# First-layer keys zero-padded to 128 rows, and conditioning products kept in one piece, in a two-layer transformer kernel

## The chip, the core and the metric

The kernel runs on one core of a Trainium2 chip. The metric is the device time of one execution in microseconds (us), from the kernel's start to its end; the time before is the median of three runs. The engines are named as in the profile: PE is TensorE with its matmuls, PEld is its weight load, DVE is VectorE, ACT is ScalarE, POOL is GpSimd, and SP issues the DMAs. PEclk is the clock that the throttle granted TensorE, as a share of full speed.

## What is computed

256 tokens of width 1024 pass two layers. Each layer has a mixer and an MLP, each with shift, scale and gate from a conditioning vector c. Cut to what the change touches:

```python
def ada_modulation(c, w, b):
    m = jax.nn.silu(c) @ w + b
    shift, scale, gate = jnp.split(m[:, None, :], 3, axis=-1)
    return shift, scale, 1.0 + gate

def mixer_ab(h, cos, sin, w_in, q_norm, w_uq, w_uiq, sinks, w_out):     # layer 0
    aq, ak, av, cq, bk, bv, bik, biw = _split_widths(h @ w_in, AB_WIDTHS)
    ...                                       # rotary embedding of queries and keys
    ya = swa_sink_attention(aq, ak, av, sinks)        # A: 8 heads, window 128, 2 key heads
    yb = dsa_attention(bq, bk, bv, biq, bik, iw)      # B: 8 heads, one key head, top 64 keys
    return jnp.concatenate([ya, yb], axis=-1) @ w_out
```

In dsa_attention an indexer first scores every key: `raw = einsum('bqhd,bsd->bhqs', iqb, ik)`, then relu, a weighted sum over 8 heads, and the 64 best keys for each query. A head has 64 numbers (HD = 64). Layer 1 has 16 ordinary heads (group C), which the change leaves as they are.

## The kernel before, in words

**Stages.** The projections of layer 0 (`group`, L615 and L635) accumulate over 8 tiles of 128 channels until about 48 us. Then the first mixer's attention runs, to about 150 us, beside the output projection `ps_out`; then the first MLP, layer 1's mixer, and the second MLP. Tokens are two blocks of 128, `b` = 0 and 1. Block 0 has 128 keys, block 1 has 256.

**Score products.** Queries and keys are transposed so that the 64 numbers of a head lie on partitions: even heads on rows 0 to 63 of a tile, odd heads on rows 64 to 127 (`half` = 0 or 1). The keys `akT`, `bkT` and `ikT` hold both halves in one tile. A product at L486 (`ps_s`, attention) or L759 (`ps_i`, indexer) takes the rows of one half of both operands, so it is a matmul of 64 rows. f32 matmuls are issued as two instructions each; the profile counts both.

**One step of attention** (`attend`) is a pair of heads: two products at L486, the mask and row minimum on DVE (L490, `negm`), Exp on ACT (L494), transposes on PE (L498), a copy on ACT (L500), and the products with the values (L505, `ps_pv`). The indexer's chain is L759 on PE, Relu on ACT (L761), and a sum on DVE (L764); `select` then runs 8 rounds of MAX and MATCH_REPLACE on DVE (L774, L775).

**Conditioning beside it.** Twelve pieces of the conditioning weights (`by_tensor`: the gate of the first half-layer, shift and scale of the second) are evaluated by PE (`ada_rows`). One piece is 8 matmuls at L334, 16 instructions, with 32 weight columns each: silu(c) in column 0 and zeros in 31, built once as `cT` of 128 x 8 x 32. The four column groups hold four partial sums; an ACT copy (L339) and two products with a column of ones (L350, `onec`) add them up. In PE's queue these products stand between the attention's own.

**What sets the order.** The tile framework's scheduler orders each engine's queue by priority, the program's order by default. `later(n)` raises the number of what is recorded inside it, so that it stands later; `ROWS_LATER` (30) is the number for `ada_rows`, L186. `st` interleaves the sides: A of block 0 beside the indexer, A of block 1 beside selection and B's queries, then B of both blocks beside `ps_out`. Weights come by DMA on SP in the order of `plan`, four buffers ahead of what has been taken.

**Buffers.** Rotary embedding writes the keys of B and the indexer into `kd`, one buffer of a tag of its own; most other work tiles of that size share the tag `r2` with 8 buffers. `ps_kd` is their transpose (L706), copied to `bkT` and `ikT` by L707 and L708.

## Time and profile before

| What | us |
|---|---|
| median of 3 runs (lowest, highest) | 728.42 (724.62, 729.69) |
| profiled execution, its own time | 719.67 |
| its span (first to last instruction) | 717.9 |
| PE busy | 674.9 (94%) |
| PEld busy | 543.8 (76%) |
| DVE busy | 473.1 (66%) |
| ACT busy | 336.2 (47%) |
| POOL busy | 67.7 (9%) |
| mean DMA rate | 211 GB/s |

The profile is of one execution. Its page gives busy time by engine, the span in 40 slices with PEclk, and groups of instructions by line. The stretch view gives, for each stretch of time, the busy time of every engine with its count of instructions in brackets, PEclk, the DMA engines' share and GB/s. The timeline gives start, length, engine, line, operation, tiles, rows x columns of the weights, shape of the streamed operand, count, and in square brackets the engine's idle time before it and what ended it. A length in the timeline runs to the modelled end of the last instruction, which overlaps the next; the distance from one start to the next start is the pace. The chain of waits shows the same work as non-overlapping pieces.

### The profile page before, as it was taken

The page shows a single profiled execution, that of the slowest core. Times are in us where ns is not written, and L with a number is a line of the kernel's source. Part 1 is how long each engine was busy: PE and PEld are TensorE (multiplying, and loading weights), DVE is VectorE, ACT ScalarE, POOL GpSimd, SP SyncE. Part 2 cuts the span into 40 slices and gives each one's busy share as a digit, 9 for nine tenths or more (in the row PEclk, how much of TensorE's full clock was granted, in tenths as well). Part 3 has the DMA queues.
Part 4 walks back from the last instruction along what each step waited for, and adds up shares of the span by engine and source line. Part 5 has one row for each costly group of instructions (what it writes and reads, how often), then busy time and mean ns, then how long its engine had stood idle before and what let it go on. Part 6 is the DMA issues. An engine that isn't in the chain of part 4 may idle for free.

```text
span 717.9 us, 9838 instructions
## 1 busy us (share of the span) xinstructions
PE 674.9 (94%) x3802; PEld 543.8 (76%) x3802; DVE 473.1 (66%) x858; ACT 336.2 (47%) x528; POOL 67.7 (9%) x85
## 2 busy tenths in 40 slices
PE   6998998999799999999978999999989999999994
PEld 3545555667689899898956877778779998989883
DVE  2855754626988877776497988854688754445537
ACT  3233333734465554545553444455546545555540
POOL 3010000003402000000043000000340010000004
PEclk9995857999999999999997999969999999999998
DMA  8991424760679898877444776731067765555301
GB/s 316 408 380 35 152 107 158 278 267 1 208 268 385 307 351 294 304 266 283 149 126 168 242 288 237 286 126 52 1 235 292 284 248 205 190 189 176 118 0 59
DMA packets 24385, 151.52 MB, mean 211 GB/s; under 512 B 2833, under 2 KB 3089, under 8 KB 8338
## 3 DMA queue, kind: packets, MB, share of 16 engines
q1 hardware_dynamic: 24194, 150.71, 57.3%
q8 instruction: 30, 0.49, 0.3%
q10 hardware_dynamic: 144, 0.18, 0.1%
q14 instruction: 17, 0.14, 0.1%
HBM read 149.83 MB, written 1.05 MB: 210 GB/s over the span
## 4 chain that ended last, share of the span: by engine, by line
PE 64%; issue 24%; DVE 7%; POOL 2%; DMA 1%; ACT 1%; SPq 0%; DVEq 0%; POOLq 0%; ACTq 0%
PE ps_m L236 16%; PE ps_m L234 16%; PE ps_m L235 16%; PE ps_g L615 3%; PE ps_s L486 2%; PE ps_ada L334 2%; PE ps_g L635 2%; PE ps_pv L505 2%; DVE wl L172 2%; PE ps_uq L727 1%; PE ps_i L759 1%; DMA early<-in_ada_dram 1%; DVE hTl L172 1%; PE ps_pt L498 1%; POOL x L588 1%
## 5 line engine op out<-in xcount | busy, mean ns | idle before, releaser
L172 DVE TENSOR_TENSOR wl<-w_w,wh 128x1024 fp32r<-128x1024 f32 x128 | 156.3, 1239 | 93.8 <-ACT wh L171 93.3
L171 ACT CAST wh<-w_w 128x1024 fp32r<-128x1024 f32 x128 | 131.1, 1052 | 154.8 <-PE ps_m L235 89.4
L234 PE MATMUL ps_m<-hTh,wh 128*128 128x256 f32 x448 | 126.7, 283 | 0.0
L236 PE MATMUL ps_m<-hTh,wl 128*128 128x256 f32 x448 | 126.6, 283 | 0.0
L235 PE MATMUL ps_m<-hTl,wh 128*128 128x256 f32 x448 | 126.6, 283 | 0.0
L234 PE MATMUL ps_m<-wh,uh 128*128 128x512 f32 x256 | 101.8, 398 | 0.0
L235 PE MATMUL ps_m<-wl,uh 128*128 128x512 f32 x256 | 101.3, 396 | 0.2 <-DVE wl L172 0.2
L236 PE MATMUL ps_m<-wh,ul 128*128 128x512 f32 x256 | 101.1, 396 | 0.0
L321 DVE CUSTOM_DVE_ANT_0 junk<-w_ada,cB,sm 128x1024 bf16<-128x1024 f32 x68 | 87.1, 1281 | 10.2 <-DMA w_ada<-in_ada_dram 9.4
L235 PEld LDWEIGHTS ps_m<-hTl,wh 128*128 128x128 f32 x448 | 85.7, 191 | 1.3
L234 PEld LDWEIGHTS ps_m<-hTh,wh 128*128 128x128 f32 x448 | 85.7, 191 | 1.2
L236 PEld LDWEIGHTS ps_m<-hTh,wl 128*128 128x128 f32 x448 | 85.7, 191 | 0.1
L236 PEld LDWEIGHTS ps_m<-wh,ul 128*128 128x128 f32 x256 | 48.2, 188 | 11.7 <-DVE ul L172 0.6
L234 PEld LDWEIGHTS ps_m<-wh,uh 128*128 128x128 f32 x256 | 48.3, 189 | 10.4 <-ACT uh L171 0.8
L235 PEld LDWEIGHTS ps_m<-wl,uh 128*128 128x128 f32 x256 | 48.2, 188 | 10.1 <-DVE wl L172 0.6
L236 PE MATMUL ps_c<-wh,hTl 128*128 128x512 f32 x96 | 39.8, 415 | 4.5 <-DVE hTl L172 4.5
L234 PE MATMUL ps_c<-wh,hTh 128*128 128x512 f32 x96 | 40.9, 426 | 3.2 <-ACT hTh L171 3.2
L235 PE MATMUL ps_c<-wl,hTh 128*128 128x512 f32 x96 | 39.5, 412 | 0.0
L171 ACT CAST wh<-w_ci 128x1024 fp32r<-128x1024 f32 x24 | 25.1, 1054 | 27.9 <-PE ps_c L236 20.1
L301 POOL TENSOR_TENSOR rs<-rs,mhalf 128x1 f32<-128x1 f32 x8 | 6.7, 832 | 333.1 <-DVE rs L573 333.1
L172 DVE TENSOR_TENSOR ul<-relu,uh 128x512 fp32r<-128x512 f32 (+1 forms) x36 | 24.8, 689 | 16.7 <-ACT uh L171 16.7
L494 ACT ACTIVATE prob<-prob,negm 128x128 f32<-128x128 f32 (+1 forms) x64 | 26.7, 453 | 18.5 <-DVE negm L490 18.5
(221 smaller groups left out, 1076.8 us busy)
## 6 DMA issues: line engine op xcount, KB each, us to landing
w_w<-in_w_dram SPq DMA_DIRECT2D x64, 1024.0 KB, 5.0
w_ada<-in_ada_dram SPq DMA_DIRECT2D x40, 1024.0 KB, 4.9
w_ci<-in_c_in_dram SPq DMA_DIRECT2D x12, 1024.0 KB, 5.0
w_ada<-in_ada_dram SPq DMA_DIRECT2D x12, 512.0 KB, 9.5
w_wo<-in_w_out_dram SPq DMA_DIRECT2D x4, 1024.0 KB, 5.6
w_co<-in_c_out_dram SPq DMA_DIRECT2D x4, 1024.0 KB, 4.9
w_g<-in_w_g_dram SPq DMA_DIRECT2D x8, 356.0 KB, 9.1
early<-in_ada_dram SPq DMA_DIRECT2D x4, 512.0 KB, 8.8
```

The source lines that it names most:

```text
L171: nc.scalar.copy(dh, src)
L172: nc.vector.tensor_sub(dl, src, dh.bitcast(F32))
L234: nc.tensor.matmul(ps, a[0], b[0], start=start, stop=False)
L235: nc.tensor.matmul(ps, a[0], b[1], start=False, stop=False)
L236: nc.tensor.matmul(ps, a[1], b[0], start=False, stop=stop)
L321: state[key, j] = nc.vector.tensor_tensor_reduce(out=junk, in0=w, in1=cB, scale=1.0, scalar=bias, op0=ALU.mult, op1=ALU.add, accum_out=m)
L334: m = nc.tensor.matmul(ps[g, :256], cT[:, k], w[:, 256 * k:256 * (k + 1)], start=k < 4, stop=k >= 4)
L486: nc.tensor.matmul(ps[:, j * 256:j * 256 + nk], qT[rows, p0 + j, b * P:(b + 1) * P], kT(p0 + j)[rows, :nk], start=True, stop=True)
L494: state["critical"] = nc.scalar.activation(pr[:, j, :nk], pr[:, j, :nk], AF.Exp, bias=negm[:, hd:hd + 1], scale=-1.0)
L505: state["pv"] = nc.tensor.matmul(pv[:, i * 65:(i + 1) * 65], flat[:, o:o + P], vv(kb, head(p0 + j, half)), start=(kb == 0), stop=(kb == b))
L615: nc.tensor.matmul(ps[b][:, :s.stop - s.start], hk[:, b * P:(b + 1) * P], w[:, s], start=k == 0, stop=k == KT - 1)
L635: nc.tensor.matmul(g1[b], hk[:, b * P:(b + 1) * P], parts["g1", k // 2][0][:, k % 2 * 512:k % 2 * 512 + 512], start=k == 0, stop=k == KT - 1)
```

## The change

Each key tile of layer 0 becomes two, one for each half, 128 rows high, with the other half's rows set to zero by POOL. Both operands of L486 (for A and B) and L759 then have 128 rows; the query rows of the wrong half meet zeros. Layer 1 keeps 64-row products. ACT fills the halves with copies of 64 partitions, two where there was one. `kd` moves to the tag `r2`. `cT` becomes 128 x 8, and a step of zero repeats each column 32 times in the weight load; all four column groups' 32 rows then hold the same partial sum, and a column `four`, which is one at rows 0, 32, 64 and 96, takes the place of `onec`. `ROWS_LATER` becomes 0.

```diff
-SPLITS_LATER, ADA_LATER, ROWS_LATER = 200, 300, 30
+SPLITS_LATER, ADA_LATER, ROWS_LATER = 200, 300, 0
...
-    cT = const.tile([P, KT, 32], F32, name="cT")
-    nc.gpsimd.memset(cT, 0.0)
-    nc.scalar.activation(cT[:, :, 0], sm[:, S_C:S_C + KT], AF.Silu)
-    onec = const.tile([P, 1], F32, name="onec")
-    nc.gpsimd.memset(onec, 1.0)
+    cT = const.tile([P, KT], F32, name="cT")
+    nc.scalar.activation(cT, sm[:, S_C:S_C + KT], AF.Silu)
...
+    four = const.tile([P, 1], F32, name="four")
+    nc.vector.tensor_reduce(out=four, in_=ident[:, ::32], op=ALU.add, axis=mybir.AxisListType.X)
...
-            m = nc.tensor.matmul(ps[g, :256], cT[:, k], w[:, 256 * k:256 * (k + 1)], start=k < 4, stop=k >= 4)
+            m = nc.tensor.matmul(ps[g, :256], cT[:, k:k + 1].to_broadcast([P, 32]), w[:, 256 * k:256 * (k + 1)], start=k < 4, stop=k >= 4)
...
-            nc.tensor.matmul(ps[:, 256 + j:257 + j], rows[:, j * P:(j + 1) * P], onec, start=True, stop=True)
+            nc.tensor.matmul(ps[:, 256 + j:257 + j], rows[:, j * P:(j + 1) * P], four, start=True, stop=True)
...
-                rows = slice(half * HD, (half + 1) * HD)
...
                 for j in range(2):
+                    rows, keys = kT(p0 + j, half)
                     nc.tensor.matmul(ps[:, j * 256:j * 256 + nk], qT[rows, p0 + j, b * P:(b + 1) * P],
-                                     kT(p0 + j)[rows, :nk], start=True, stop=True)
+                                     keys[rows, :nk], start=True, stop=True)
...
-    bkT = work.tile([P, 256], F32, name="bkT")
-    ikT = work.tile([P, 256], F32, name="ikT")
+    akT, bkT, ikT = ([work.tile([P, 256], F32, name=n + str(half)) for half in range(2)] for n in ("akT", "bkT", "ikT"))
+    for kT in (akT, bkT, ikT):
+        for half in range(2):
+            nc.gpsimd.memset(kT[half][(1 - half) * HD:(2 - half) * HD], 0.0)
...
-        kd = work.tile([P, 2, 2, HD], F32, name="kd", tag="kd", bufs=1)
+        kd = work.tile([P, 4, 2, HD], F32, name="kd", tag="r2", bufs=8)[:, :2]
...
-        nc.scalar.copy(bkT[:, q], ps[:, :P])
-        nc.scalar.copy(ikT[:, q], ps[:, P:2 * P])
+        for half in range(2):
+            rows = slice(half * HD, (half + 1) * HD)
+            nc.scalar.copy(ikT[half][rows, q], ps[rows, P:2 * P])
+        for half in range(2):
+            rows = slice(half * HD, (half + 1) * HD)
+            nc.scalar.copy(bkT[half][rows, q], ps[rows, :P])
...
-        to_T([kr[:, :2].rearrange("p h d -> p (h d)")], akT[:, b * P:(b + 1) * P].rearrange("p (n q) -> p n q", n=1))
+        ps = pc("ps_T")
+        nc.tensor.transpose(ps[:, :P], kr[:, :2].rearrange("p h d -> p (h d)"), ident)
+        for half in range(2):
+            rows = slice(half * HD, (half + 1) * HD)
+            nc.scalar.copy(akT[half][rows, b * P:(b + 1) * P], ps[rows, :P])
...
-                    nc.tensor.matmul(ps[:, j * 256:j * 256 + nk], iqT[rows, p0 + j, b * P:(b + 1) * P],
-                                     ikT[rows, :nk], start=True, stop=True)
+                    nc.tensor.matmul(ps[:, j * 256:j * 256 + nk], iqT[:, p0 + j, b * P:(b + 1) * P],
+                                     ikT[half][:, :nk], start=True, stop=True)
...
-        yield from attend(b, aqT, lambda p: akT, lambda kb, hd: vA[:, kb, hd // 4], mA[:, P:] if b == 0 else mA,
+        yield from attend(b, aqT, lambda p, half: (slice(0, P), akT[half]), lambda kb, hd: vA[:, kb, hd // 4], mA[:, P:] if b == 0 else mA,
...
-        yield from attend(b, bqT, lambda p: bkT, lambda kb, hd: vB[:, kb], mB[:, b, :P * (b + 1)], ys[b][:, 512:],
+        yield from attend(b, bqT, lambda p, half: (slice(0, P), bkT[half]), lambda kb, hd: vB[:, kb], mB[:, b, :P * (b + 1)], ys[b][:, 512:],
...
-            yield from attend(b, qT, lambda p: kT[:, p], lambda kb, hd: vv[:, kb, hd], mC[:, P:] if b == 0 else mC,
+            yield from attend(b, qT, lambda p, half: (slice(half * HD, (half + 1) * HD), kT[:, p]), lambda kb, hd: vv[:, kb, hd], mC[:, P:] if b == 0 else mC,
```

The scheduler's order moves with it. Three places matter below. The change shifts the line numbers by one to ten: L487 is L486 of before, L333 is L334, L349 is L350, L734 is L727, L449 is L450.

The first place is PE at the first conditioning piece (`w_ada_8`), between the score products of A's block 0. Before:

```order
L486 MATMUL ps_s<-akT,aqT 128x128
L334 MATMUL ps_ada<-w_ada_8_288,cT 32x256
L486 MATMUL ps_s<-akT,aqT 128x128
L334 MATMUL ps_ada<-w_ada_8_288,cT 32x256 x7
L486 MATMUL ps_s<-akT,aqT 128x128 x2
L350 MATMUL ps_ada<-onec,adarows 128x1 x2
```

Now:

```order
L333 MATMUL ps_ada<-w_ada_8_287,cT 32x256 x8
L487 MATMUL ps_s<-akT_372,aqT 128x128 x2
L487 MATMUL ps_s<-akT_371,aqT 128x128
L349 MATMUL ps_ada<-four,adarows 128x1 x2
L487 MATMUL ps_s<-akT_371,aqT 128x128
```

The eight products of the piece stand together, ahead of the two score products that stood among them. `akT_371` and `akT_372` are the two halves' tiles.

The second place is PE where B's queries are projected (`ps_uq`, L727). Before:

```order
L334 MATMUL ps_ada<-w_ada_1_584,cT 32x256
L727 MATMUL ps_uq<-w_uq,cqT 128x512 x2
L334 MATMUL ps_ada<-w_ada_1_584,cT 32x256 x7
L350 MATMUL ps_ada<-onec,adarows 128x1 x2
L466 MATMUL ps_T<-ident,qr 128x128 x4
```

Now:

```order
L333 MATMUL ps_ada<-w_ada_1_597,cT 32x256 x8
L734 MATMUL ps_uq<-w_uq,cqT 128x512 x2
L349 MATMUL ps_ada<-four,adarows 128x1 x2
L465 MATMUL ps_T<-ident,qr 128x128 x4
```

Seven products that stood behind the projection, while DVE embeds its result (`qr`), now stand ahead of it.

The third place is DVE where the keys are embedded; this print shows the semaphores that a row waits for, by the engine that raises them. Before:

```order
L450 TENSOR_TENSOR kd<-rope_404,rope_405 128x2x64
L447 TENSOR_TENSOR rope_420<-g_358,sinT 128x2x32
L448 TENSOR_TENSOR rope_420<-g_358,sinT 128x2x32
L446 TENSOR_TENSOR rope_441<-evac,cosT 128x128 [waits DVE_49,Activation_49]
L447 TENSOR_TENSOR rope_442<-evac,sinT 128x2x32
L448 TENSOR_TENSOR rope_442<-evac,sinT 128x2x32
L743 COPY vA<-evac 128x2x64
L450 TENSOR_TENSOR kd<-rope_419,rope_420 128x2x64 [waits DVE_49,PE_49]
```

Now:

```order
L449 TENSOR_TENSOR kd<-rope_413,rope_414 128x2x64
L445 TENSOR_TENSOR rope_430<-g_357,cosT 128x128
L446 TENSOR_TENSOR rope_431<-g_357,sinT 128x2x32 [waits DVE_49]
L447 TENSOR_TENSOR rope_431<-g_357,sinT 128x2x32
L750 COPY vA<-evac 128x2x64 [waits Activation_49]
L449 TENSOR_TENSOR kd<-rope_430,rope_431 128x2x64 [waits DVE_49]
L449 TENSOR_TENSOR kd<-rope_430,rope_431 128x2x64
L445 TENSOR_TENSOR rope_453<-evac,cosT 128x128 [waits PE_49]
```

The wait for PE has moved from the second block's `kd` to the first rotary product of A's keys, which stands right behind it. SP's queue has the same DMAs in the same order.

More of the change, by code (lines that the diff above doesn't have):

```diff
@@ L719, in trunk @@
     bqT = work.tile([P, 1040], F32, name="bqT", tag="vv", bufs=2)[:, :1024].rearrange("p (n q) -> p n q", n=4)
-    akT = work.tile([P, 256], F32, name="akT")
     hf = lambda t: t.rearrange("p (h q) d -> p h q d", h=2)
@@ L754, in index @@
             for half in range(2):
-                rows = slice(half * HD, (half + 1) * HD)
                 ps = pb("ps_i")
```

## The prediction, made before the changed kernel had run

> **What bounds the kernel now.** I read the page's slices first, then stretches cut where the granted clock changes, then the timeline inside them.
>
> ```profile
> PEclk9995857999999999999997999969999999999998
> ```
>
> ```profile
> 57.41:77.84 20.43, 19.96 (x87) 12.34 (x87) 9.43 (x39) 6.07 (x16) 0.00 (x0) 0.50 0.16 56
> 77.84:91.55 13.71, 11.45 (x83) 7.33 (x83) 11.15 (x52) 5.72 (x14) 0.00 (x0) 1.00 0.57 216
> 91.55:108.60 17.05, 17.05 (x64) 9.26 (x65) 7.87 (x36) 4.60 (x11) 0.97 (x5) 0.50 0.19 70
> 108.60:112.02 3.42, 2.01 (x23) 1.34 (x16) 2.05 (x8) 0.37 (x1) 0.00 (x0) 1.00 0.43 117
> 112.02:118.83 6.81, 6.81 (x24) 4.28 (x23) 2.87 (x6) 3.75 (x6) 0.00 (x0) 0.50 0.23 95
> 118.83:140.00 21.17, 18.58 (x135) 11.68 (x133) 12.49 (x44) 13.30 (x28) 0.13 (x1) 1.00 0.66 254
> ```
>
> The columns are the stretch, its length, busy PE, PEld, DVE, ACT and POOL, PEclk, DMA share and GB/s. Layer 0's attention has three stretches at exactly half clock, 20.43 + 17.05 + 6.81 = 44.29 us, in which PE is busy all the time while DVE and DMA are not. There PE bounds the kernel, and its clock bounds PE. All these lengths are multiples of 3.41 us (6, 4, 5, 1, 2), so the clock is decided once in 3.41 us.
>
> What decides it is not whether PE is busy: it is, and stays at half. I tried the share of the array that the work in one such window fills.
>
> ```profile
> 53.83 0.63 PE L466 MATMUL ps_T<-ident,qr 128*128 128x128 f32 x4
> 55.13 0.71 PE L486 MATMUL ps_s<-akT,aqT 64*128 64x128 f32 x4 [0.68 <-ACT aqT L467]
> 55.82 0.63 PE L466 MATMUL ps_T<-ident,qr 128*128 128x128 f32 x4
> 57.12 0.99 PE L759 MATMUL ps_i<-ikT,iqT 64*128 64x128 f32 x4 [0.68 <-ACT iqT L467]
> ...
> 74.66 1.94 PE L334 MATMUL ps_ada<-w_ada,cT 128*32 128x256 f32 x16
> 76.53 1.78 PE L759 MATMUL ps_i<-ikT,iqT 64*128 64x256 f32 x6
> ...
> 91.22 1.79 PE L486 MATMUL ps_s<-akT,aqT 64*128 64x256 f32 x4 [0.42 <-DVE negm L490]
> 92.95 1.11 PE L498 MATMUL ps_pt<-ident,prob 128*128 128x128 f32 x4
> 93.99 1.22 PE L486 MATMUL ps_s<-akT,aqT 64*128 64x256 f32 x2
> ...
> 123.00 0.63 PE L466 MATMUL ps_T<-ident,qr 128*128 128x128 f32 x4 [1.01 <-DVE qr L450]
> 123.46 0.60 PE L498 MATMUL ps_pt<-ident,prob 128*128 128x128 f32 x4
> 123.99 0.71 PE L486 MATMUL ps_s<-bkT,bqT 64*128 64x128 f32 x4
> 124.63 0.44 PE L498 MATMUL ps_pt<-ident,prob 128*128 128x128 f32 x2
> 125.00 0.70 PE L486 MATMUL ps_s<-bkT,bqT 64*128 64x256 f32 x2
> ```
>
> ```profile
> 467.87 0.71 PE L486 MATMUL ps_s<-ckT__3632,cqT__3631 64*128 64x128 f32 x4 [0.86 <-DVE negm L490]
> 468.68 0.84 PE L498 MATMUL ps_pt<-ident,prob 128*128 128x128 f32 x4
> 469.69 1.39 PE L486 MATMUL ps_s<-ckT__3632,cqT__3631 64*128 64x128 f32 x8 [0.17 <-DVE negm L490]
> ```
>
> ```profile
> 46.39 1.73 PE ps_g L635 x4
> 83.07 1.00 PE ps_ada L334 x16
> 84.44 0.63 PE ps_s L486 x2
> 134.82 0.63 PE ps_s L486 x4
> ```
>
> At full clock L635 streams 512 columns in 1.73/4 = 0.43 us, so 256 take 0.215 and 128 take 0.107. I weight each instruction by rows x columns over 128 x 128 and count those that start in the window. The window 53.99 to 57.41 holds seven transposes (0.75) and about 5.4 half-row products (0.29): 1.04/3.41 = 0.30, and the clock falls. From 74.48: 16 x 0.215/4 + 5 x 0.215/2 = 1.40, share 0.41, and the clock rises. From 91.55: 5 x 0.107 + 4 x 0.107 = 0.96, share 0.28, and it stays low. From 122.26: ten transposes (1.07) and 0.43 of products, share 0.44, and it stays high. From 467.00: four transposes and ten products, 0.97, share 0.28, and it falls (slice 27 of PEclk). So the bound lies between 0.30 and 0.41, with rows counted: without them the window at 467 would have 0.44 like the one that stayed high. The 74.48 window needs its L334 products, 31 of whose 32 columns were zeros; zeros count.
>
> **The change part by part.** The sum is made on the profiled execution, 719.67 us. The runs' median is 8.75 higher; the profile doesn't show why, and I carry the difference.
>
> *Rows.* With 128 rows the window at 53.99 has 1.33/3.41 = 0.39, that at 91.55 has 1.50/3.41 = 0.44. Most half-clock windows should go. A stretch of PE work at half clock takes half as long at full clock, if PE is then as busy as from 77.84 to 91.55, 11.45/13.71 = 0.835 (DVE is 0.81 there, so both are near their limits). Stretch one: 19.96/2/0.835 = 11.95, 8.48 saved. Two: 8.53/0.835 = 10.21, 6.84 saved. Three: 3.41/0.835 = 4.08, 2.73 saved. Sum 18.05.
>
> ```profile
> 90.37 0.44 PE L498 MATMUL ps_pt<-ident,prob 128*128 128x128 f32 x2 [1.39 <-ACT prob L494]
> ```
>
> Two places stay thin: PE waiting behind `select` on DVE (here), and behind the embedding of B's queries (123.00 above, 1.01 idle). The second gets thinner, since the seven products that filled it now run ahead of L727. I leave two windows at half clock; each costs 3.41 - 1.71/0.835 = 1.37, so 2.7 is given back (none to six windows: 0 to 8.2). Net gain 15.3.
>
> *Row switching.* A run of two 64-row products takes 0.63 (84.44) where 128-row ones would take 0.43: about 0.10 for each change of row count. The timeline has 27 runs from 55.13 to 136.37, 46 of their 54 ends against 128-row work; the other eight meet L334 and keep their switch. That is 4.6 at full clock. Against it, products of both halves can overlap: four take 0.63 at 134.82, half of 4 x 0.215 plus switches.
>
> ```profile
> L486 PE MATMUL ps_s<-akT,aqT x32: 269/418/792, 55.1 to 100.1; 64*128 64x128 f32 x16, 64*128 64x256 f32 x16
> L486 PE MATMUL ps_s<-bkT,bqT x32: 272/376/580, 112.8 to 136.7; 64*128 64x128 f32 x16, 64*128 64x256 f32 x16
> L759 PE MATMUL ps_i<-ikT,iqT x32: 345/450/792, 57.1 to 79.3; 64*128 64x128 f32 x16, 64*128 64x256 f32 x16
> L334 PEld LDWEIGHTS ps_ada<-w_ada,cT x192: 106/110/177, 65.0 to 150.2; 128*32 128x32 f32 x192
> ```
>
> All 96 products are 48 x 0.107 + 48 x 0.215 = 15.4 of streaming; overlap lost is between nothing and half, 7.7. In the timeline 12 products start within 10 ns of the one before, six of each width: 1.9. I take 4.6 - 1.9 = 2.7, of which 2.0 shows at PE's share of 0.835 (ends: -3.1 and 4.6).
>
> [...]
>
> *Conditioning.* Kept together, a piece is 1.00 for 16 instructions (83.07), as the unsplit ones are now; five splits fewer are within the 2.0. The zero step's weight load isn't in the trace: nearest is the load of 32 columns, 0.110, which hides today under a pace of 1.00/16 = 0.062. If it costs the same, 0; if each load shows in full, 16 x 0.110 - 1.00 = 0.76 a piece, 9.1 for twelve; a gain has no mechanism, as the columns stay 32. I take 0.
>
> *Copies, zeros, kd.*
>
> ```profile
> 50.98 0.49 DVE L450 TENSOR_TENSOR kd<-rope,rope 128x128 f32<-128x128 f32 x2 [1.24 <-PE ps_kd L706]
> 54.49 0.58 ACT L467 COPY aqT<-ps_T 128x512 f32<-128x512 f32 x1 [1.82 <-PE ps_T L466]
> L707 ACT COPY bkT<-ps_kd x2: 266/268/269, 51.0 to 52.1; 128x128 f32<-128x128 f32 x2
> 20.00:40.00 20.00, 20.00 (x60) 11.15 (x59) 16.73 (x40) 5.29 (x11) 0.00 (x0) 1.00 1.03 409
> ```
>
> The second block's `kd` waited 1.24 for the first block's transposes. With more buffers the wait isn't gone: by the order (third place) it moves to the next rotary product. Two `kd` instructions (0.41) and a copy now run ahead of it that ran behind, and three rotary products went the other way. Ends: 0 and 1.24; I take 0. ACT gets seven more copies at most 0.27 each by the nearest row: 1.9 uncovered; they lie in front of 54.49, where ACT idled 1.82, or beside the second block. I take 0. POOL's six memsets run while POOL idles (the last row has 0.00), long before PE's first use at 55.13; `four` is a DVE instruction of at most 0.25 (half of the `kd` row) while the first weights load. Nothing here adds a wait for PE but the one on POOL's zeros.
>
> Sum: 15.3 + 2.0 = 17.3. The profiled execution goes to 702.4, the median to 711.1.
>
> **The rivals.** *Something else is last once the clock is up* (0.20). DVE is busy 0.81 of the one full-clock stretch in the middle, and in the new order eight rounds of `select` are as many as before. If PE falls to 0.6 busy, stretch one saves 20.43 - 16.63 = 3.80, two 17.05 - 14.21 = 2.84, three 2.73; less 2.7 and plus 2.0 gives 8.7: 719.8. Against it: from 77.84 to 91.55 both engines reached over 0.8 together.
>
> *More windows than the profile has* (0.15). If the median's 8.75 above the profiled execution is half-clock windows, they are 8.75/1.37 = 6.4, and go too: 702.4. Nothing in the profile shows them.
>
> *The clock doesn't follow the added rows* (0.08): zeros in rows may not count, or my bound may be a coincidence of five windows. Then only switching is left: 726.4. Against it stand the zero columns of L334 at 74.48.
>
> *Transposes don't count* (0.06). Then the window at 53.99 goes from 0.08 to 0.17 and still falls, and that at 91.55 from 0.16 to 0.31 and stays; I give it one window of the thirteen, 1.4, and switching 2.0: 725.0. Against it: without transposes the window at 122.26 had 0.13 and stayed high, less than the 0.16 at 467.00 that fell. [...]
>
> *Slower: the zero step's loads* (0.06). If reading one column 32 times stops the loads of the four column groups from hiding, and each takes the longest of its row, 0.177, ahead of its 0.062, a piece takes 16 x 0.239 = 3.82 instead of 1.00. Twelve pieces add 33.9 on PE, in stretches that PE bounds; less 17.3 that is 16.6 slower: 745.0. It decides from (17.3/12 + 1.00)/16 = 0.153 per instruction. Nothing in the trace speaks for it but that no row has such a load.
>
> **How the numbers follow.** The forecast has 0.45: 711.1, its own range 704 to 717 by the residual windows (none to six) and switching. A measurement of this kernel can tell about 1% from no change, 7.3 us, so faster begins at 721.1. Faster: the forecast, the higher gain, and 0.15 of the first rival's 0.20, together 0.75. Same: the clock and transpose rivals with what is left of the first, 0.19. Slower 0.06. The range is 700 to 725: it takes in the forecast, the first two rivals and the transpose one, and leaves out 0.14 and some of the tails.
>
> **What would show it.** Right: PEclk at 0.9 or above in slices 4 to 7 with at most two or three windows at 0.50 between 54 and 120; PE busy near 0.83 there; L487 and L769 rows at 128*128, a run of two in about 0.43; L333 still 1.00 for 16; everything from the output projection on the same, only about 17 us earlier. A window of half-row work at 0.28 that now runs on at full clock shows the bound. Wrong: half clock in the same places with 128-row products (rows or zeros don't count); full clock with PE idle behind DVE `mx` and `score` (first rival); L333 slower than 0.15 each (the loads); or a gain at full clock in the attention that a later stage gives back, by new half-clock windows around 370 to 390 and 467 to 485, whose place in the window the shift moves.

## The result, and the profile after

| What | before | changed |
|---|---|---|
| median of the runs made together, us | 726.52 (720.30 to 729.69, 4 runs) | 695.95 (694.85 to 710.33, 4 runs) |
| ratio, 95% interval | | 0.9584 (0.9499 to 0.9670) |
| median of all executions in this study, us | 724.6 (713.8 to 732.4, 36) | 700.6 (694.9 to 711.3, 8) |
| profiled execution, its span | 719.67, 717.9 | 695.99, 694.2 |

The changed kernel is faster: 30.6 us in the runs made together, 24 over all executions. The forecast was 17.3 us and 711.1, with a range of 700 to 725: the sign was right, the forecast gain was too small, and the runs made together lie below the range, while the median of all executions is just inside it. The ratios leave out executions over 1.5% above the fastest of their kernel; the medians of all executions keep them, because the spread itself is part of what has to be explained.

The slices of the changed kernel's page, the row of the granted clock, and the stretches cut where it changes (columns as in the prediction):

```profile
PEclk9999869999999999999988999999999999999997
```

```profile
55.23:82.53 27.30, 22.53 (x181) 17.02 (x181) 24.04 (x101) 12.75 (x34) 0.00 (x0) 1.00 0.43 155
82.53:96.19 13.66, 13.15 (x63) 8.88 (x64) 6.67 (x31) 4.55 (x11) 1.14 (x5) 0.50 0.29 97
96.19:99.60 3.41, 1.58 (x10) 1.04 (x9) 2.38 (x8) 0.00 (x0) 0.00 (x0) 1.00 0.56 233
99.60:103.01 3.41, 3.41 (x18) 3.13 (x16) 1.09 (x5) 2.73 (x6) 0.00 (x0) 0.50 0.00 0
103.01:120.08 17.07, 15.84 (x127) 12.18 (x127) 11.62 (x42) 11.14 (x24) 0.00 (x0) 1.00 0.67 251
448.08:461.15 13.07, 11.94 (x86) 9.09 (x84) 10.41 (x35) 11.47 (x25) 0.00 (x0) 1.00 0.52 185
```

The reader is to see three things. The first 27 us of the attention, up to the wait behind `select`, are now at full clock with PE busy 22.53/27.30 = 0.83; they hold the work of before's first stretch of half clock. Half clock is left in two places, 13.66 + 3.41 = 17.07 us, where 44.3 were: they are the places of before's second and third stretch, so the second, 17.05 long before, has shrunk by one window only. And the last row is layer 1's attention, which the change does not touch: it is at full clock here and was at half for 13.65 us before.

The timeline where the clock falls, at 82.53:

```profile
74.51 0.60 PE L487 MATMUL ps_s<-akT,aqT 128*128 128x256 f32 x2
74.95 0.27 PE L499 MATMUL ps_pt<-ident,prob 128*128 128x128 f32 x1
...
76.42 1.07 PE L333 MATMUL ps_ada<-w_ada,cT 128*32 128x256 f32 x16
77.42 0.70 PE L487 MATMUL ps_s<-akT,aqT 128*128 128x256 f32 x2
...
80.96 1.13 PE L487 MATMUL ps_s<-akT,aqT 128*128 128x256 f32 x4 [1.74 <-DVE negm L491]
81.92 0.38 PE L499 MATMUL ps_pt<-ident,prob 128*128 128x128 f32 x2
83.04 1.97 PE L506 MATMUL ps_pv<-vA,probT 128*128 128x65 f32 x8 [0.73 <-ACT probT L501]
84.94 1.94 PE L333 MATMUL ps_ada<-w_ada,cT 128*32 128x256 f32 x16
```

A run of two score instructions now takes 74.95 - 74.51 = 0.44, the 0.43 that was forecast instead of 0.63, and a conditioning piece is still 1.00 for sixteen instructions (76.42 to 77.42). PE waits 1.74 for DVE before 80.96; that is the thin window that drops the clock, behind `select`, where the prediction had one of its two. By the prediction's count the window from 79.11 to 82.53 has four score instructions and two transposes, a share of 0.31. The next one, from 82.53 to 85.94, has 0.31 as well although PE is busy for 2.90 of its 3.41 us: eight value instructions (L506) stream only 65 columns each, and twelve conditioning instructions count a quarter. No score product starts in that window, so there is nothing in it to add rows to.

Where the 23.7 us between the two profiled executions came from, by the start of the last product of each stage in the trace: 18.5 by the end of layer 0's attention with its output projection (178.74 against 160.24), 18.45 by the end of the first MLP, 17.5 by the end of layer 1's projections, and then 23.8 by the end of layer 1's output projection: 6.3 us more in a stage that has the same instructions as before.

### The profile page after: what moved, and what is told of

The parts are those of the page before. It is cut to its first block, busy times and chain, and to the rows that moved or that the text cites. A ratio compares the mean times of both kernels' runs of the same rounds, so it can differ in the third digit from the quotient of the medians.

```text
span 694.2 us, 9843 instructions
## 1 busy us (share of the span) xinstructions
PE 649.9 (94%) x3802; PEld 535.6 (77%) x3802; DVE 474.0 (68%) x859; ACT 337.4 (49%) x534; POOL 67.3 (10%) x89
## 4 chain that ended last, share of the span: by engine, by line
PE 63%; issue 24%; DVE 8%; POOL 2%; ACT 1%; DMA 1%; SPq 0%; DVEq 0%; POOLq 0%; ACTq 0%
PE ps_m L236 17%; PE ps_m L234 16%; PE ps_m L235 16%; PE ps_g L616 3%; PE ps_g L636 2%; PE ps_s L487 2%; DVE wl L172 2%; PE ps_pv L506 1%; PE ps_ada L333 1%; PE ps_uq L734 1%; DMA early<-in_ada_dram 1%; POOL x L589 1%; DVE hTl L172 1%; PE ps_i L769 1%; POOL rs L300 1%
## 5 line engine op out<-in xcount | busy, mean ns | idle before, releaser
L171 ACT CAST wh<-w_w 128x1024 fp32r<-128x1024 f32 x128 | 131.2, 1052 | 154.8 <-PE ps_m L235 89.4
L172 DVE TENSOR_TENSOR wl<-w_ci,wh 128x1024 fp32r<-128x1024 f32 x24 | 31.2, 1308 | 7.4 <-ACT wh L171 7.1
```

Of the source, the lines that this page charges most:

```text
L171: nc.scalar.copy(dh, src)
L172: nc.vector.tensor_sub(dl, src, dh.bitcast(F32))
```

## The experiments

**The kernel before, once more.** No edit.

> The kernel before, once more, with its profile, to see what of its time is the lottery of the 3.41 us window. Theory (share of the array in a window decides the clock, and where the windows fall is chance): half-clock stretches again in layer 0's attention, 35 to 50 us in all, but of other lengths and starts; in layer 1's attention near 467 to 484 either none or one of 3.4 to 14 us; times between 718 and 731. Rival (the stretches belong to the program alone): the same stretches to within a window, layer 1's too, and times within 0.3%.

Measured: 725.15 us, ratio 1.0064 (0.9933 to 1.0194). Its profiled execution ended layer 0's attention at 188.86 instead of 178.74. A stretch that the first profile does not have:

```profile
121.35:135.01 13.66, 12.65 (x92) 8.34 (x84) 6.61 (x31) 7.29 (x16) 0.00 (x0) 1.00 0.85 306
135.01:158.90 23.89, 22.91 (x109) 14.57 (x108) 9.90 (x27) 9.46 (x19) 0.13 (x1) 0.50 0.70 264
```

The same instructions ran at half clock for 23.89 us more here, seven windows of 3.41 us more in layer 0 than in the first profile (68.27 against 44.37 us; 35 to 50 were expected). The length from the last projection to the end of the attention grew by 140.23 - 131.22 = 9.0 us: 0.38 us for each us at half clock. So the 8.75 us between the first profile and the median are half clock, and the number of windows is different in each execution. The mean clocks on record agree: over 32 executions of this kernel the time follows the half clock, taken as 2 x (1 - mean clock) x span, with 0.35 us for each us and a correlation of 0.94.

**The changed kernel, once more.** No edit.

> The changed kernel once more, unchanged. Theory (a free-running 3.41 us window decides the clock from rows times streaming time, so each execution meets the thin places at another phase): the median stays at 694 to 700 with single executions up to 711, and a profile whose half-clock stretches differ from the first one's: layer 0 keeps one stretch of 7 to 20 us that begins between 79 and 90, and layer 1's attention (448 to 462 us) is at half clock in some executions, 6 us each. Rival (layer 1 is 6.3 us shorter for a reason of the change itself): its attention is at full clock in every execution, 13 us long, and all executions are within 2 us.

Measured: 705.08 us (699.66 to 711.27), ratio 0.9762 (0.9655 to 0.9869). Its profiled execution took 711.27:

```profile
58.24:65.07 6.83, 6.26 (x37) 5.42 (x39) 3.54 (x12) 3.07 (x8) 0.00 (x0) 0.50 0.00 0
85.55:99.20 13.65, 13.56 (x64) 8.88 (x64) 6.25 (x28) 4.13 (x11) 1.15 (x5) 0.50 0.33 110
102.62:109.45 6.83, 6.83 (x37) 4.54 (x35) 2.87 (x6) 4.12 (x7) 0.00 (x0) 0.50 0.00 0
129.92:140.16 10.24, 9.75 (x60) 5.89 (x53) 1.93 (x10) 3.27 (x8) 0.00 (x0) 0.50 0.98 378
461.02:478.09 17.07, 17.07 (x69) 13.99 (x70) 7.28 (x29) 7.54 (x19) 0.00 (x0) 0.50 0.38 124
```

Layer 0 has 37.55 us at half clock here, and layer 1's attention, at full clock in the first profile, has 17.07 and takes 55.33 us from the last projection to the last output product instead of 47.56. One program, two executions, 15 us apart. The spread was expected. The median was expected at 694 to 700, and layer 0 at no more than 20 us of half clock. The difference lies in where the windows fall. Just before the drop the two traces have the same instructions at the same distances; the window from 457.60 to 461.01 of this one has a share of 0.33 to 0.35 by the prediction's count, and the lowest window of the other execution in that place, 447.76 to 451.17, has 0.44.

**The changed kernel with 64-row products in layer 0.** The padded tiles stay; the products use one half of them.

```diff
-                    nc.tensor.matmul(ps[:, j * 256:j * 256 + nk], iqT[:, p0 + j, b * P:(b + 1) * P],
-                                     ikT[half][:, :nk], start=True, stop=True)
+                    nc.tensor.matmul(ps[:, j * 256:j * 256 + nk], iqT[half * HD:(half + 1) * HD, p0 + j, b * P:(b + 1) * P],
+                                     ikT[half][half * HD:(half + 1) * HD, :nk], start=True, stop=True)
```

(and `slice(half * HD, (half + 1) * HD)` in place of `slice(0, P)` for `akT` and `bkT`)

> The changed kernel with its score products of layer 0 taking 64 rows again, all else as changed (one piece of conditioning, zero step, order of the queues almost the same). Theory (the added rows hold the clock): half clock comes back for 30 us or more between 57 and 120, PE busy there, and the time is 715 to 728. Rival (the new order or the conditioning brought the gain): half clock stays at 17 us or less in layer 0 and the time is 695 to 705.

Measured: 715.19 us, ratio 0.9912 (0.9761 to 1.0063).

```profile
57.20:74.27 17.07, 16.60 (x82) 10.66 (x81) 8.74 (x38) 5.80 (x15) 0.00 (x0) 0.50 0.18 63
87.92:104.99 17.07, 16.05 (x69) 10.15 (x70) 8.54 (x39) 5.05 (x12) 1.15 (x5) 0.50 0.31 103
```

Half clock is back where it was before the change, 51.20 us of it in layer 0, against 17.07, 37.55 and 30.72 in the three profiles that have the changed kernel's layer 0. One profile would not be enough for this, as the spread shows, but the mean clocks agree: 0.928 to 0.949 in these four executions, 0.948 to 0.973 in seven of the changed kernel's eight (0.927 in the eighth, whose 695.91 us doesn't go with such a clock). The rows hold the clock up. Its profiled execution was 7.7 us shorter than before's all the same; 6.3 of them are layer 1's attention, which fell at full clock.

**The kernel before with each 64-row score product of layer 0 issued twice.**

```diff
-                    nc.tensor.matmul(ps[:, j * 256:j * 256 + nk], qT[rows, p0 + j, b * P:(b + 1) * P],
-                                     kT(p0 + j)[rows, :nk], start=True, stop=True)
+                    for _ in range(1 if side[:1] == "c" else 2):
+                        nc.tensor.matmul(ps[:, j * 256:j * 256 + nk], qT[rows, p0 + j, b * P:(b + 1) * P],
+                                         kT(p0 + j)[rows, :nk], start=True, stop=True)
```

(and so in the indexer)

> The kernel before with each 64-row score product of layer 0 issued twice, so that PE does more work and nothing else is changed. It adds the share that the zero rows add, without 128-row products. Theory (share decides the clock): the windows at 0.25 to 0.30 rise to 0.37 or more, half clock in layer 0 shrinks from 44 us to 25 or less, and the time is 3 to 12 us below the kernel before in spite of the 7.7 to 15 us of added PE work. Rival (fewer row switches, or a shorter PE queue, made the change fast): it is slower than before by 7 to 16 us, and half clock stays at 40 us or more.

Measured: 730.71 us, ratio 1.0116 (0.9964 to 1.0268).

```profile
57.29:91.42 34.13, 34.07 (x129) 21.89 (x129) 13.11 (x53) 7.19 (x20) 0.00 (x0) 0.50 0.17 62
```

A miss: more products did not bring the clock back, and PE ran ten windows on end at half clock without idling. The reason is in the size of the thing: 64-row products one after the other at half clock fill at most 64/128 x 0.5 = 0.25 of a window, however many there are. That is below the bound, so they can't raise the clock by themselves; the next experiment tests this.

**Streams of one kind.** Each stream starts after some 8 us of idle PE: 64 rows; 128 rows and then 64; 128 rows of which 64 are zeros; the two halves in turn; transposes; 128 rows and 32 columns.

```diff
+    for todo in ([(half_rows, 24)], [(all_rows, 20), (half_rows, 30)], [(zero_rows, 30)], [(both_halves, 40)],
+                 [(transposes, 100)], [(columns, 24)]):
```

> No model: six streams of PE products on arbitrary data with PE idle for some 12 us ahead of each; the output is a copy of x. (1) 24 products of 64 rows, one half alone; (2) 20 products of 128 rows and behind them without a pause 30 of 64 rows; (3) 30 of 128 rows with zeros in the lower half of the keys; (4) 40 of 64 rows, the halves in turn; (5) 100 transposes; (6) 24 products of 32 columns on one column group. Theory (share of rows x columns at a bound between 0.30 and 0.41): (1) can fill 0.25 at half clock and stays at half to its end, 0.43 us an instruction; (2) rises within two windows, and its 64-row part then stays at full clock, 0.215 an instruction, since it fills 0.5 there; (3) rises like (2), zeros count; (4) rises; (5) rises, transposes count; (6) fills 0.125 and stays at half. Rival (busy time decides): all six rise within two windows. Rival (transposes or zeros don't count): (5) or (3) stays at half.

The timeline of the first three streams. The records of the clock begin at 49.57 in this trace, so the pace tells it: 256 columns of f32 take 0.43 us at half clock and 0.21 at full.

```profile
14.36 20.85 PE L108 MATMUL ps<-key,x 64*128 64x256 f32 x48 [14.36 <-DVE key L103]
44.05 11.61 PE L112 MATMUL ps<-key,x 128*128 128x256 f32 x40 [8.85 <-DVE key L103]
55.59 13.21 PE L108 MATMUL ps<-key,x 64*128 64x256 f32 x60
```

64 rows stay at half clock to their end (20.85/48 = 0.43), with PE never idle. The same instruction behind 128-row work runs at full clock (13.21/60 = 0.22). The next stretches are 128 rows of which 64 are zeros, transposes, and products of 32 columns:

```profile
78.46:83.70 5.24, 5.24 (x12) 4.20 (x13) 0.42 (x2) 0.00 (x0) 0.50 0.00 0
83.70:94.20 10.50, 10.50 (x49) 8.93 (x47) 0.00 (x0) 0.00 (x0) 1.00 0.00 0
123.07:128.08 5.01, 5.01 (x24) 5.01 (x25) 0.32 (x1) 0.00 (x0) 0.50 0.00 0
128.08:133.00 4.92, 4.92 (x47) 4.92 (x46) 0.00 (x0) 0.00 (x0) 1.00 0.01 3
144.87:148.56 3.69, 3.69 (x9) 1.61 (x10) 0.00 (x0) 0.00 (x0) 0.50 0.00 0
148.56:157.00 8.44, 8.44 (x40) 4.18 (x38) 0.00 (x0) 0.00 (x0) 1.00 0.00 0
```

All three rise within two windows. (The two halves in turn, which start in pairs 0.01 apart and take 0.21 an instruction at half clock, rise too, at 107.60 after 4.6 us; the kernel was not tried with its halves in turn.) Zeros in rows count: 128 rows of which 64 are zeros rose after 5.24 us, 64 rows alone not in 20.85. These f32 transposes count: they rose after 5.01 us. And 32 columns count as much as 128, a miss of the theory, and not as the prediction weighted them: they rose after 3.69 us, where a quarter weight gives them 0.125 of a window. Rows times the time in which the array streams is the count that fits all six streams. L334's quarter weight was the right number for another reason: its four column groups stream at the same time, 16 instructions in 1.00 us where one alone takes 0.21.

**Streams of 72 to 112 rows.**

```diff
+    for r in (72, 80, 88, 96, 112, 64):
...
+            nc.tensor.matmul(ps[:, :256], x0[:r, :P], k[:r], start=True, stop=True)
```

> No model: six streams of 88 products of 256 f32 columns, back to back, each after about 8 us of idle PE, with 72, 80, 88, 96, 112 and 64 rows. All start at half clock, where a stream without gaps fills rows/128 x 0.5 of a window: 0.281, 0.313, 0.344, 0.375, 0.438 and 0.25. Theory (rows in use are counted, bound between 0.31 and 0.40): 64 and 72 stay at half clock to their end (0.43 us an instruction), 112 rises within two windows, 80 to 96 tell the bound. Rival (rows are counted by the size of the row group that is switched on, 64 or 128): all but the one of 64 rise alike. Second rival (rows don't matter above 64): the same picture as the first rival.

```profile
14.30 37.91 PE L108 MATMUL ps<-key,x 72*128 72x256 f32 x88 [14.30 <-DVE key L103]
61.06 37.91 PE L108 MATMUL ps<-key,x 80*128 80x256 f32 x88 [8.84 <-DVE key L103]
107.81 37.91 PE L108 MATMUL ps<-key,x 88*128 88x256 f32 x88 [8.85 <-DVE key L103]
154.58 22.43 PE L108 MATMUL ps<-key,x 96*128 96x256 f32 x88 [8.85 <-DVE key L103]
185.84 22.15 PE L108 MATMUL ps<-key,x 112*128 112x256 f32 x88 [8.84 <-DVE key L103]
216.25 37.91 PE L108 MATMUL ps<-key,x 64*128 64x256 f32 x88 [8.26 <-DVE key L103]
```

72, 80 and 88 rows stay at half clock for all 37.91 us (0.43 an instruction), like 64; 96 and 112 rise after some 7 us, an estimate from the lengths: (22.43 - 88 x 0.215)/0.215 = 16 instructions at 0.43, and 15 by 22.15. Groups of 16, 32 or 64 rows would count 88 and 96 alike, so rows in use are counted more finely than that, and at half clock the bound lies between 88/256 = 0.344 and 96/256 = 0.375. Both rivals fall.

**The changed kernel with the conditioning products free to be split again.**

```diff
-SPLITS_LATER, ADA_LATER, ROWS_LATER = 200, 300, 0
+SPLITS_LATER, ADA_LATER, ROWS_LATER = 200, 300, 30
```

> The changed kernel with ROWS_LATER at 30 again, so that the conditioning products may be split by score products as before; rows and zero step stay. In the executions profiled so far the end of layer 0's attention rises by about 0.40 us for each us at half clock in it; at no half clock the changed kernel would end it at 153.4, the changed kernel with 64-row products (rows64) at 156.5, the kernel before at 161.0. Theory (the 4 to 5 us between rows64 and before come from the conditioning kept together, which drops row switches and waits): with 30 the end less 0.40 times its half clock is 156 to 158, and the median is 702 to 708. Rival (they come from the zero step, kd or the order of the keys' copies): 153 to 154, and the median as the changed kernel's, 696 to 705.

Measured: 704.88 us (701.98 to 708.88), ratio 0.9750 (0.9691 to 0.9809). Its first piece, which the score products of one head split:

```profile
62.48 0.62 PE L333 MATMUL ps_ada<-w_ada,cT 128*32 128x256 f32 x2
63.03 0.49 PE L487 MATMUL ps_s<-akT,aqT 128*128 128x128 f32 x2
63.45 1.06 PE L333 MATMUL ps_ada<-w_ada,cT 128*32 128x256 f32 x14
64.44 0.71 PE L487 MATMUL ps_s<-akT,aqT 128*128 128x128 f32 x4
```

The two instructions ahead take 63.03 - 62.48 = 0.55, the fourteen behind 64.44 - 63.45 = 0.99, together 1.54; in the changed kernel the sixteen take 1.00. A split costs 0.54 us at full clock: the two run alone, and the fourteen behind them take as long as sixteen did. This kernel runs the twelve pieces in 18 parts, the changed one in 12: 6 x 0.54 = 3.2. At equal half clock the attention's end is 3.0 later (table below). The theory held; its median alone would not have told, as it lies within the spread.

The next table has every profiled execution with layer 0 unfilled: the length D from the last projection's start to the last output product's start, the time H at half clock within it, and D - 0.40 H, the length at full clock (0.38 from the two of before, 0.43 from those of the changed kernel).

| kernel | D | H | D - 0.40 H |
|---|---|---|---|
| before, two executions | 131.2, 140.2 | 44.4, 68.3 | 113.5, 112.9 |
| changed, 64-row products | 129.8 | 51.2 | 109.3 |
| changed, `ROWS_LATER` 30 | 117.1 | 20.5 | 108.9 |
| changed, three executions (the third is the next experiment's, whose layer 0 is the same) | 112.4, 121.2, 118.3 | 17.1, 37.6, 30.7 | 105.5, 106.1, 106.0 |

**Padded keys in layer 1's second head group too.** Layer 0's key tiles and `cqT` become one tile `kpad`, which holds the eight padded key tiles of that group once layer 0 is done.

```diff
+    kpad = work.tile([P, 2, 4, 256], F32, name="kpad")
+    cqT = kpad[:, :, 3]
+    akT, bkT, ikT = ([kpad[:, half, n] for half in range(2)] for n in range(3))
...
+                nc.scalar.copy(kpad[rows, half, :, b * P:(b + 1) * P], ps[rows].rearrange("p (n q) -> p n q", q=P))
...
-            yield from attend(b, qT, lambda p, half: (slice(half * HD, (half + 1) * HD), kT[:, p]), lambda kb, hd: vv[:, kb, hd], mC[:, P:] if b == 0 else mC,
+            yield from attend(b, qT, lambda p, half: (slice(0, P), kpad[:, half, p]) if g else (slice(half * HD, (half + 1) * HD), kT[:, p]), lambda kb, hd: vv[:, kb, hd], mC[:, P:] if b == 0 else mC,
```

> The changed kernel with the keys of layer 1's second group zero-padded to 128 rows too, in the key tiles of layer 0 and the query tile that are free by then (one tile holds them all); layer 0 keeps its instructions and order. Theory: the thin stretch at 448 to 462 us fills more of each window (at least 0.40), so no execution is at half clock there; the median is 0 to 4 us below the changed kernel's in the same job, the highest execution at least 4 below its highest. Cost: two more ACT copies of 64 partitions and some row switching gone, between -1 and +1 us. Rival (layer 1's gain had nothing to do with the clock there): same as the changed kernel within 1 us, spread as wide.

Measured: 696.15 us (691.54 to 700.87), ratio 0.9663 (0.9575 to 0.9752). Layer 1's attention takes 45.47 us, at full clock, where the changed kernel took 47.56 at full clock and 55.33 with half clock. No profiled execution with this padding (four, with those below) had half clock there. So layer 1's 6.3 us come from half clock, in a stage that the change does not touch. The median is 8.9 below the changed kernel's in the same set of runs, more than the 4 expected. Of the 2.1 at equal clock, row switches account for some 0.9 (changes of row count in this stage fall from 15 to 4, at the 0.08 each found below); the rest is open.

**Useless products where PE waits.** Identity times silu(c), into parts of PSUM that nothing reads before they are written again.

```diff
+    def filler(dst, after):
+        for _ in range(2):
+            m = nc.tensor.matmul(dst, ident, cB[:, :dst.shape[1]], start=True, stop=True)
...
+                if side == "a1" and p0 and not half:
+                    filler(state["w11"][:, 258:], "s")
...
+        if fill:
+            filler(ps[:, :256], "uq")
```

> The changed kernel with six products added that compute nothing that is used: identity times silu(c), 254 to 256 columns of f32, two in front of the value products at 82 us, two each behind the projections of B's queries, where PE idles behind DVE. Each is 0.43 us at full clock, 2.6 in all. Theory: they lift the thin windows at 79 to 86 and 96 to 103 us over 0.37, so the half clock there shrinks from 17 us to at most 7, layer 0's attention ends 2 to 5 us earlier, and so does the kernel. Rival (DVE sets the pace there, the clock doesn't matter): half clock gone but the attention's end the same within 1 us or up to 2.6 later. Second rival (phase decides more than filling): half clock as long as before.

Measured: 691.93 us (688.18 to 696.72), ratio 0.9608 (0.9521 to 0.9695). The timeline at the thin place and the stretches of the attention:

```profile
81.62 1.13 PE L498 MATMUL ps_s<-akT,aqT 128*128 128x256 f32 x4 [1.74 <-DVE negm L502]
82.80 1.06 PE L464 MATMUL ps_ada<-cB,ident 128*128 128x254 f32 x4
83.70 1.10 PE L517 MATMUL ps_pv<-vA,probT 128*128 128x65 f32 x8
```

```profile
55.00:82.00 27.00, 22.25 (x182) 16.82 (x182) 23.74 (x98) 12.68 (x33) 0.00 (x0) 1.00 0.42 152
82.00:103.00 21.00, 20.61 (x163) 14.94 (x164) 16.04 (x62) 10.27 (x20) 0.97 (x5) 1.00 0.60 207
445.22:462.29 17.07, 17.07 (x69) 14.08 (x69) 7.16 (x27) 7.42 (x20) 0.00 (x0) 0.50 0.37 128
```

PE waits the same 1.74 us for DVE, but the 0.9 us of filling behind it carry the clock over the window's end, and the eight value products that took 1.97 take 1.10. Layer 0's attention has no half clock left, here and in the three other profiles with these products (below); it ends at 151.89, 8.4 us earlier than in the changed kernel's first profile, where 2 to 5 were expected. At 0.40 a us, the 17.07 us of half clock make only 6.8; the length D is 103.3, 2.2 to 2.8 below the table's length at full clock, so the last windows cost more than 0.40 or the products do something else too. Layer 1, not filled, fell to half clock in this execution.

**Both together.** The two diffs above in one kernel, in two sets of runs.

> Padded keys in layer 1's second group and the six added products together. Theory: both effects add, 2 to 8 us below the changed kernel's median in the same job: 688 to 694, and the narrowest spread of the four, under 6 us. Rivals as for the two alone: same as the changed kernel within 2 us.

> The kernel with padded keys in both layers and the six added products again, on the same chip: 684 to 689 as before, all half clock outside 345 to 385 us and the last 10 us at most two windows.

Measured: 686.62 us (684.27 to 688.80), ratio 0.9526 (0.9447 to 0.9606), a little below the 688 to 694 expected; again, 685.60 (683.96 to 687.15). This beats the changed kernel by 14 us in the medians of all executions, and its eight executions lie within 5 us where the changed kernel's eight spread over 16. The row of the granted clock:

```profile
PEclk9999999999999999999989999999999999999997
```

**Filling in layer 1's projections too.** Twelve more such products where PE waits 4.0 and 1.8 us for DVE and ACT.

```diff
+        if warm == 0:
+            f = filler(pb("ps_f")[:, :256], "c", 8)
```

> The kernel with padded keys in both layers and the six added products, and twelve more of them at the start of layer 1's projections, where PE waits 4.0 and 1.8 us for ACT and DVE: eight behind the second product of the first accumulation (3.4 us at full clock), four in front of the second token block's. Every execution profiled so far is at half clock for 6.8 to 10.2 us between 345 and 385 us, in projections that fill every row and that PE bounds. Theory (a window is judged by its share of rows times streaming time, whoever supplies it): at most 3.4 us of half clock are left there, and the projections end 2 to 4 us earlier: 682 to 685 in the median. Rival (the idle time belongs to DVE's chain, which sets the end there whatever the clock): the same as the kernel without them within 1 us, or up to 1.5 slower where the products run into the wait's end.

Measured: 689.07 us (685.58 to 689.93) beside 685.60 without them. The theory missed. The rival's mechanism was right, and its size wasn't: it allowed 1.5 us, and 3.5 came. First the kernel with both (its second set of runs), then this one, around the wait:

```profile
351.07 0.80 PE L236 MATMUL ps_c<-wh,hTl 128*128 128x512 f32 x1 [4.03 <-DVE hTl L172]
351.66 0.63 PE L234 MATMUL ps_c<-wh,hTh 128*128 128x512 f32 x1
```

```profile
347.29 3.61 PE L475 MATMUL ps_f<-cB,ident 128*128 128x256 f32 x16
350.98 0.40 PE L236 MATMUL ps_c<-wh,hTh 128*128 128x512 f32 x1
356.46 1.43 PE L428 MATMUL ps_mod<-ident,z 128*128 128x128 f32 x8 [3.00 <-DVE z L606]
```

The clock is held (0.40 an instruction instead of 0.63 in the rows behind the wait, half clock there 3.41 instead of 10.24 us), and what PE gains it waits for again at 356.46, 3.00 us behind DVE. The projections' last product starts at 439.77 against 439.74. Why this kernel's executions are then some 3 us longer is not settled. Its profiled one was its shortest and doesn't show it; layer 1's attention took 46.61 against 45.47 us there.

## Why the prediction was right or wrong

The forecast of 711.1 lies 15.2 us above the 695.95 measured. 8.75 of them are the difference between profile and median that was carried, and 6.4 are the profiled execution, 695.99 where 702.4 was forecast; nearly all of these 6.4 are layer 1's attention. The windows, row switching and conditioning of layer 0 had errors of their own, which cancel.

**What bounds the kernel: right.** The clock in layer 0's attention, decided by rows in windows of 3.41 us. The bound of 0.30 to 0.41 holds 0.344 to 0.375. It holds in the kernels too: with rows times the streaming time that lies inside each window, counted over the 1792 windows between 50 and 560 us of the twelve traces of whole kernels, 166 of which are followed by half clock, all but 5 of those below 0.344 or above 0.375 are followed by half or full clock as the bound says. The weight by columns was wrong, and with it the argument that L334's zero columns count; that zeros in rows count was tested by itself.

**Rows, 15.3: right in price, wrong in number.** A window of half clock was priced at 1.37; measured, 3.41 x 0.40 = 1.36. "I leave two windows at half clock" is where it failed: five stayed in the first profile, eleven and nine in two others. The prediction judged the second stretch by its first window, which 128 rows lift to 0.44; the windows behind `select` have 0.31, and the value products and conditioning in them gain no rows. Between the two first profiles eight windows went, 10.9 us, not eleven net.

**Row switching, 2.0: too small.** Between 64-row and 128-row products in the same order the length at equal clock falls by 109.3 - 105.9 = 3.4. Changes of rows or columns from one PE instruction to the next fall from 72 to 28 between these two kernels in that stage, so a change is worth 0.08 net. At the 0.10 priced the 44 are 4.4, which leaves some 1.0 for lost overlap; 1.9 had been taken off for it, and PE's share besides, where 0.835 of 2.7 would have been 2.25 and not 2.0.

**Conditioning kept together, 0: wrong.** "Five splits fewer are within the 2.0" should have been a term of its own: 0.54 a split, 3.0 in all. The rest of the step was right: the zero step's weight loads take what the loads took before, 106/110/177, and the piece is still 1.00:

```profile
L333 PEld LDWEIGHTS ps_ada<-w_ada,cT x192: 105/110/177, 61.9 to 129.8; 128*32 128x32 f32 x192
```

**Copies, zeros, kd, 0: right to 0.3.** A's first score product starts 0.66 later than before (55.79 against 55.13), of which 0.39 came with the projections' end.

**Sum for layer 0: right by errors that cancel.** 10.9 for the clock and 113.5 - 105.5 = 8.0 for the rest are 18.9, 18.5 with the later start; 15.3 and 2.0 were forecast.

**Everything behind on the same: wrong.** It held to the end of layer 1's projections (17.5). Layer 1's attention then gave 6.3 that the change has no part in: half clock there depends on where the windows fall, and came up in six of the eight profiled executions that have 64-row keys there: all three of the kernel before, the one with doubled products included, and three of the five built on the changed kernel. The prediction had named a shift of windows only as a loss.

**"The profile doesn't show why, and I carry the difference": the step that cost most.** The 8.75 between the first profile and the median were half-clock windows, which the second profile of before has, and the change removes part of them. That was the second rival, at 0.15, and its 702.4 lies within 2 us of the 700.6 of all executions; that it is so near is partly luck, since it lets all the extra windows go and takes layer 1 as it was. Taken over the few profiled executions, the clock in layer 0 gives 0.40 x (56.3 - 28.5) = 11.1 and the rest 113.2 - 105.9 = 7.3: 18.4 of the 24. Most of what is left is half clock too. By the mean clocks on record, half clock in the whole execution averages 92 us before and 55 in seven of the changed kernel's eight (without the one at 0.927), 36 less, of which 28 lie in layer 0 by the profiles; the other 8 make some 3 us in the stages behind. Whether the change makes half clock rarer there, or the few executions do, stays open, and so do the last 2 us. That the four runs made together came out at 695.95, and not near the 700.6 of all, is luck of the windows.

The other rivals fell: DVE became the limit only in places (0.88 busy from 55 to 82, PE 0.83), the clock follows rows (88 stay at half, 96 rise), transposes count (they rose after 5.01 us), and the zero step's loads stay hidden (1.00 a piece).

## What to carry to other kernels

Where PE is busy at half clock, add up rows times streaming time over a window: 64-row products one after the other did not raise the clock in 37.91 us, while a contraction padded with zeros did after 5.24 us, and a few useless products in a wait held it (no half clock left in layer 0 in four profiles). Both paid where PE bounds the stage (51.20 us at half clock in layer 0 with 64-row products, 17.07 to 37.55 with padded ones; 8.4 us less with the filling); added products did not where DVE bounds it (689.07 against 685.60). A stage near the bound came out differently in each execution (17.1, 37.6 and 30.7 us at half clock in the same layer 0), so take several profiles, express each stage at equal half clock, and do not carry a difference between a profile and a median as a constant. Price each interruption of overlapping column groups (0.54 us here) as a term of its own.

## What the runs showed of the hardware

- The clock's window weighs the rows in use, zeros included: 88 of 128 rows streaming without a gap stayed at half clock for 37.9 us, 96 rose after some 7 us, and 128 of which 64 were zeros after 5.24. 64 rows behind 128-row work kept full clock (0.22 us an instruction for 13.21 us). Columns did not enter: 32 rose after 3.69 us.
- f32 transposes raised the clock as well, after 5.01 us: 24 at 0.21 us, then 0.105.
- A us at half clock cost 0.38 to 0.43 us of time in layer 0's attention, between executions of one layer 0.
- Sixteen instructions in four column groups took 1.00 us in one piece and 1.54 in two.
- The same program differed by 15 us, 2% of its time, between two executions by where the windows fell. They keep no fixed place in the program: the first half clock of layer 0 begins 9.90 us behind the last projection's start in one execution of before and 11.28 in the other, which is not a multiple of 3.41 apart.
